# A two-branch gated-attention layer: phase 1 keeps the high and low parts of h in DRAM, and phases 2 and 3 load them

## The chip, the cores and the metric

The kernel runs on one core of one Trainium2 chip. The metric is the time of one launch on the device, in microseconds, as the median of several runs. The engines are named as in the profile: PE (matrix products) and PEld (loading its weights), DVE (VectorE), ACT (ScalarE), POOL (GpSimd), and SP (SyncE), whose queue issues nearly all transfers here. Each engine carries out its instructions in the order in which they stand in its queue, and waits where one of them needs something that another engine or a transfer has not delivered.

## The reference

One layer of a streaming encoder, for a prompt of 4096 tokens and 64 sample tokens, model width 1024, all in fp32. What is computed, cut to the core:

```python
mod = c @ w_ada + b_ada
shift, scale, gate = split(mod, 3)
h = rms_norm(x, g_pre) * (1 + scale) + shift
q_a, k_a, v_a, z_a, a_lr, q_h, f_h, i_h, z_h = split(h @ w_in)
o_a, s_a = chunked_gla(q_a, k_a, v_a, log_sigmoid(a_lr @ w_alpha + b_alpha) / 16, s_gla)
f = lb + (1 - lb) * sigmoid(f_h)
o_h, s_h = chunked_gla(silu(q_h), 1 - f, i_h, log(f), s_hgrn)
o_a = rms_norm(o_a, g_on_gla) * silu(z_a)
o_h = rms_norm(o_h, g_on_hgrn) * silu(z_h)
y = x + gate * rms_norm(concat(o_a, o_h) @ w_out, g_post)
```

So one input h feeds three groups of projections: those of the GLA branch, those of the HGRN2 branch, and the gate path z_h. The two recurrences carry a state from chunk to chunk.

## The kernel before, in words

A core does not hold all the split weights of `w_in` and `w_out` at once, so the work is done in three phases over the same tokens. The prompt is cut into 16 groups of 256 tokens, each of two tiles of 128; the 64 sample tokens ride with group 15 in phase 1 and with group 2 in phases 2 and 3, and that group has 320 columns.

An fp32 product is made of three matmuls on a high and a low part: hi·hi, hi·lo and lo·hi. `split` (L86) makes the two parts: ACT casts the source to the high part (L92), DVE subtracts it from the source to give the low part (L93). The same two lines split the weights, on DVE or on POOL. h of one group lies in SBUF as four tiles, each with two of the eight slices of the width: as fp32 in the tiles `hf` (pool of 4 buffers), and split in the tiles `hh` (pool of 5).

- **Setup** computes the modulation and makes h of group 0 directly as split tiles `h0` and as `hf`.
- **Phase 1** walks over the groups. For each it does the GLA projections (`proj_gla`, with L607 and L619 as the matmul lines). Woven between them, by generators with due times (`weave`), are the recurrence of the group before (`attend_group`) and the preparation of the next group: `x_load` brings x in 32 small loads (L486), `quad_norm` takes its norm (squares on ACT, L514; the sum over partitions as a small product on PE, L517; the scaling on DVE, L520), `x_turn` transposes it on DVE (L556) and applies scale and shift on ACT and DVE (L563, L565), which gives `hf`; then it stores `hf` to `h_d` in DRAM (L568). At the end of the group `split_h` (L579) makes the next group's `hh`.
- **Phase 2** walks over the groups again, with the HGRN2 projections and recurrence. `load_hf` (L572) brings `hf` back for the next group, and `split_h` splits it once more.
- **Phase 3** walks over the token tiles: the z projection (`z_tile`, L619), the turning of the gated outputs (L1300) and the out-projection (L1335). `load_hf` and `split_h` do the same a third time. Its weights `w_out` are loaded and split, on DVE, ACT and POOL, at the end of phase 2.

The order inside each engine's queue is set by a scheduler from the order of the code, the due times of the generators and its own estimate of lengths; the buffers of a pool decide when a tile may be written. Other lines that come up: L1156 scales a chunk's output on DVE and L1157 stores it to `oa_d` or `oh_d`; L850 updates the state S on DVE, which L823 on PE reads; L909 prepares K and staging tiles on DVE, which L766 and L956 read; L1263 loads `og`, the stored outputs, in phase 3, L1286 x, and L1351 stores y; L1253 loads w_out; L442 and L446 compute the gate rows in phase 2, from loads of L435.

Of the kernel before, what the change touches and what calls it, by code (L numbers as in the profile page):

```python
# [6 lines left out]
F32 = mybir.dt.float32  # L7
F32R = mybir.dt.float32r
# [20 lines left out]
class Kernel:  # L29
# [105 lines left out]
    def setup(self):  # L135
# [12 lines left out]
        for g, tl in enumerate(self.groups):  # L148
            self.h_d.append(dram.tile([P, KT, GROUP], F32, name=f"h_d{g}"))
            self.oa_d.append([dram.tile([r, 512], F32, name=f"oa_d{g}_{j}") for j, (_, _, r, _) in enumerate(tl)])  # L150
            self.oh_d.append([dram.tile([r, 512], F32, name=f"oh_d{g}_{j}") for j, (_, _, r, _) in enumerate(tl)])
        self.h_s = dram.tile([P, KT, self.dec], F32, name="h_s")
        self.gate_d = dram.tile([2, D], F32, name="gate_d")
# [62 lines left out]
    def first_group(self, ap, ada, w, rows):  # L216
# [110 lines left out]
        ada_sum(pa, parts.pop(0), [(1, 0), (1, 1)])  # L327
        self.hf = [self.hp.tile([P, 2, T], F32, name="hf", bufs=4) for _ in range(4)]
        nc.vector.tensor_copy(col[:, 16:], pr[:, 16:52])
# [6 lines left out]
        parts[1] = [ada_split(sts[1][0], nc.gpsimd)]  # L336
        self.h0 = [self.hp.tile([P, 2, 2, T], F32R, name="hh", bufs=5) for _ in range(4)]
        ada_turn(0, am)
# [149 lines left out]
    def x_norm(self, g, js):  # L488

        nc = self.nc  # L490
        ss = self.small.tile([P, 2], F32, name="x_ss")
        for i, j in enumerate(js):
            xt, r = self.xs[j], self.groups[g][j][2]
            junk = self.hp.tile([P, 2, GROUP], F32, name="hf", bufs=4).rearrange("p k c -> p (k c)")
# [27 lines left out]
    def x_turn(self, g):  # L522
# [3 lines left out]
        T = self.tokens(tl)  # L526
        self.hf = hf = [self.hp.tile([P, 2, T], F32, name="hf", bufs=4) for _ in range(4)]
        for tiles, cnd in (([0, 1], 0), ([2], 1)):
# [23 lines left out]
            for i in range(4):  # L552
# [13 lines left out]
                yield  # L566
        for i in range(4):
            nc.sync.dma_start(self.h_d[g][:, 2 * i : 2 * i + 2, :], hf[i][:, :, :GROUP])  # L568
            if len(tl) == 3:
                nc.sync.dma_start(self.h_s[:, 2 * i : 2 * i + 2, :], hf[i][:, :, GROUP:])  # L570

    def load_hf(self, g, tl):  # L572
        self.hf = [self.hp.tile([P, 2, self.tokens(tl)], F32, name="hf", bufs=4) for _ in range(4)]
        for i in range(4):
            self.nc.sync.dma_start(self.hf[i][:, :, :GROUP], self.h_d[g][:, 2 * i : 2 * i + 2, :])
            if len(tl) == 3:
                self.nc.sync.dma_start(self.hf[i][:, :, GROUP:], self.h_s[:, 2 * i : 2 * i + 2, :])

    def split_h(self):  # L579

        out = []
        T = self.hf[0].shape[2]
        for i in range(4):
            u = self.hp.tile([P, 2, 2, T], F32R, name="hh", bufs=5)
            self.split(u[:, 0], u[:, 1], self.hf[i])
            out.append(u)
        return lambda k: out[k // 2][:, :, k % 2]

# [791 lines left out]
    def run(self):  # L1380
# [11 lines left out]
        with ExitStack() as rec:  # L1392
            self.open_recurrence(rec)
            self.setup_late()
            for i in range(4):
                nc.sync.dma_start(self.h_d[0][:, 2 * i : 2 * i + 2, :], self.hf[i])
            h = lambda k: self.h0[k // 2][:, :, k % 2]
            S, Ss = [None], [t["state_gla"]]
# [10 lines left out]
            def prep_h(g, tl):  # L1409
                self.load_hf(g, tl)  # L1410
                yield

            for g in range(ng):
                prep = prep_x(g + 1) if g + 1 < ng else prep_h(0, self.groups2[0])
                sides = [(side, 12, 1, 18), (prep, 8, 0, 16) if g == 0 else (prep, 8, 7, 19)]
                if g == ng - 1:

                    sides.append((self.weights(W2["f"], C_FH, 512, "wu"), 10, 8, 18))
                    sides.append((self.weights(W2["q"], C_QH, 512, "wv"), 10, 20, 26))
                res = self.weave(self.proj_gla(g, h), sides)  # L1420
                h = self.split_h()
                side = self.attend_group(g, S, Ss, res, 2, 2, self.oa_d, t["new_gla_p"], t["new_gla_s"])
# [4 lines left out]
            for g in range(ng):  # L1427
# [113 lines left out]
```

## Time and profile before

| what | value |
|---|---|
| median of 3 runs | 2156.19 us (2154.54 to 2158.08) |
| the profiled execution | 2154.41 us, of which its span 2152.6 |
| granted PE clock, mean | 0.996 |
| bytes moved by DMA | 173.22 MB, mean 80 GB/s |
| phase 1, one group | 44.785 us |
| phase 3, one token tile | 17.3 us |

The profile is one execution, and all times in it are microseconds from its start, unless marked as nanoseconds. A row of a group names line, engine, operation and tiles, then the count, the busy time, the mean length of one in nanoseconds, and the idle time just ahead of these instructions with what ended most of it. A row of the list of waits names the waiting engine, its tile and line, what it waited for, and total, number and longest. In a timeline a bracket holds the idle time ahead of the row and what ended it.

### The profile page before, as it was taken

What the parts mean: (1) busy time and instruction counts of PE and PEld (TensorE: products, weight loads), DVE (VectorE), ACT (ScalarE), POOL (GpSimd) and SP (SyncE); (2) the same over time, 40 slices, a digit from 0 to 9 for tenths busy, and PEclk for the clock granted to TensorE, in tenths of its full rate; (3) what the DMA queues carried; (4) which work ended last, traced back from release to release, by engine and by line L of the source; (5) the groups of instructions that cost most, each with busy time, mean ns of one, the idle gap of its engine ahead of it and who ended that gap; (6) DMA issues with size and microseconds to landing.
All of it is one profiled execution on the core that took longest, in us unless ns stands there. A gap on an engine that the chain in (4) does not pass through costs nothing.

```text
span 2152.6 us, 44904 instructions
## 1 busy us (share of the span) xinstructions
PE 2108.6 (98%) x16574; PEld 1849.9 (86%) x16574; DVE 1492.5 (69%) x4851; ACT 996.1 (46%) x2960; POOL 239.8 (11%) x640
## 2 busy tenths in 40 slices
PE   8999999999999999999999999999989999999998
PEld 6888989889898888989999898999868888888887
DVE  6777767777677787677788777677995454545444
ACT  6666655665556664444444444444542222222212
POOL 3200010001100111110111111000330000000000
PEclk9999999999999999999999999999999999999999
DMA  9322222222222321112211111011343333333322
GB/s 274 102 63 71 61 56 50 72 66 58 55 50 64 118 87 39 38 33 71 66 50 50 31 31 50 31 31 48 98 150 132 118 123 108 127 117 131 108 100 88
DMA packets 218632, 173.22 MB, mean 80 GB/s; under 512 B 136236, under 2 KB 158224, under 8 KB 218412
## 3 DMA queue, kind: packets, MB, share of 16 engines
q1 hardware_dynamic: 218268, 170.08, 26.8%
q8 instruction: 131, 2.15, 0.4%
q14 instruction: 89, 0.73, 0.1%
q10 hardware_dynamic: 144, 0.26, 0.0%
HBM read 118.35 MB, written 51.93 MB: 79 GB/s over the span
## 4 chain that ended last, share of the span: by engine, by line
PE 85%; DVE 8%; ACT 4%; issue 1%; DMA 1%; POOL 0%; SPq 0%; DVEq 0%; ACTq 0%; POOLq 0%
PE ps_pj L619 23%; PE ps_pj L607 22%; PE ps_pj L1335 16%; PE ps_at L619 7%; PE ps_at L686 2%; PE ps_ms L839 2%; PE ps_o L823 2%; PE ps_o L818 2%; PE ps_at L956 2%; PE ps_at L766 1%; DVE wst L909 1%; PE ps_tp L793 1%; ACT A L776 1%; PE ps_tp L1300 1%; PE ps_ms L1300 1%
## 5 line engine op out<-in xcount | busy, mean ns | idle before, releaser
L619 PE MATMUL ps_pj<-wu,hh 128*128 128x512 f32 x1632 | 410.7, 398 | 4.3 <-DVE hh L93 3.4
L607 PE MATMUL ps_pj<-hh,wu 128*128 128x256 f32 (+1 forms) x2976 | 392.3, 287 | 0.0
L607 PEld LDWEIGHTS ps_pj<-hh,wu 128*128 128x128 f32 x2976 | 372.9, 191 | 4.9 <-issue 0.3
L619 PEld LDWEIGHTS ps_pj<-wu,hh 128*128 128x128 f32 x1632 | 296.4, 188 | 66.0 <-DVE hh L93 3.9
L607 PE MATMUL ps_pj<-hh,wv 128*128 128x256 f32 (+1 forms) x1536 | 214.1, 289 | 0.0
L607 PEld LDWEIGHTS ps_pj<-hh,wv 128*128 128x128 f32 x1536 | 192.5, 188 | 14.9 <-issue 12.9
L619 PE MATMUL ps_pj<-wv,hh 128*128 128x264 f32 x1464 | 199.3, 290 | 1.9 <-DVE wv L93 1.9
L619 PEld LDWEIGHTS ps_pj<-wv,hh 128*128 128x128 f32 x1464 | 184.2, 188 | 7.1 <-issue 2.3
L1340 ACT ACTIVATE sq<-ps_pj 128x512 bf16<-128x512 f32 (+1 forms) x66 | 39.4, 597 | 294.7 <-PE ps_pj L1335 293.2
L1335 PE MATMUL ps_pj<-wv,ogh 128*128 128x512 f32 x512 | 162.2, 397 | 0.0
L1335 PE MATMUL ps_pj<-wu,ogh 128*128 128x512 f32 x512 | 158.0, 390 | 0.0
L619 PE MATMUL ps_at<-wu,hh 128*128 128x512 f32 x672 | 157.4, 390 | 0.0
L92 ACT CAST hh<-hf 128x512 fp32r<-128x512 f32 (+1 forms) x188 | 117.3, 626 | 68.6 <-PE ps_pj L619 37.0
L619 PEld LDWEIGHTS ps_at<-wu,hh 128*128 128x128 f32 x672 | 126.0, 188 | 26.1
L1201 ACT ACTIVATE g<-ps_pj 128x256 f32<-128x256 f32 (+1 forms) x128 | 49.4, 386 | 200.2 <-PE ps_pj L607 199.8
L93 DVE TENSOR_TENSOR hh<-hf,hh 128x512 fp32r<-128x512 f32 (+1 forms) x188 | 132.5, 711 | 6.5 <-ACT hh L92 5.5
L909 DVE TENSOR_TENSOR wst<-wst,T 128x160 f32<-128x160 f32 (+4 forms) x480 | 118.4, 265 | 4.0
L1335 PEld LDWEIGHTS ps_pj<-wu,ogh 128*128 128x128 f32 x512 | 96.1, 188 | 20.8
L938 POOL COPY T<-T 128x16 f32<-128x16 f32 (+1 forms) x32 | 9.9, 309 | 931.4 <-DVE Qg L879 827.8
L1335 PEld LDWEIGHTS ps_pj<-wv,ogh 128*128 128x128 f32 x512 | 93.8, 188 | 19.1
L1335 PE MATMUL ps_pj<-wv,ogl 128*128 128x512 f32 x256 | 100.5, 393 | 0.0
L1335 PE MATMUL ps_pj<-wu,ogl 128*128 128x512 f32 x256 | 99.7, 390 | 0.0
(303 smaller groups left out, 3758.5 us busy)
## 6 DMA issues: line engine op xcount, KB each, us to landing
hf<-h_d SPq DMA_DIRECT2D x128, 256.0 KB
xt<-in_x_prompt_dram SPq DMA_DIRECT2D x36, 512.0 KB
h_d<-hf SPq DMA_DIRECT2D x64, 256.0 KB
out_y_prompt_dram<-y SPq DMA_DIRECT2D x31, 512.0 KB
xt<-in_x_prompt_dram SPq DMA_DIRECT2D x448, 32.0 KB
wst<-in_w_in_dram SPq DMA_DIRECT2D x36, 256.0 KB
ada_st<-in_w_ada_dram SPq DMA_DIRECT2D x32, 256.0 KB
oa_d<-e SPq DMA_DIRECT2D x32, 256.0 KB
```

What stands on the lines that cost most here:

```text
L92: self.nc.scalar.copy(hi, src)
L93: (eng or self.nc.vector).tensor_tensor(lo, src, hi.bitcast(F32), ALU.subtract)
L607: self.nc.tensor.matmul(ps[:, :T], a, b, start=i == 0, stop=i == n - 1)
L619: self.nc.tensor.matmul(ps[:r, : c1 - c0], a, b, start=kt == 0 and i == 0, stop=kt == KT - 1 and i == 2)
L686: nc.tensor.transpose(pt[:, i * P : (i + 1) * P], D[:, c + i, :], self.ident)
L818: nc.tensor.matmul(po[h], A[:, c * 4 + h, :], v, start=h < n, stop=St is None and h == 4 - n)
L823: nc.tensor.matmul(o, Q[rows[s], c * G + g, :], St[rows[s], g, :], start=NS == 2 and not apart and h == 1, stop=h == 4 - NS or h == 3 and ...
L839: nc.tensor.matmul(pd[s * w : (s + 1) * w, g, :], kc[:CL, g, s * w : (s + 1) * w], vs[c][:CL, h * P : (h + 1) * P], start=not apart, stop= ...
L909: nc.vector.tensor_tensor(parts(dst), parts(src), t.unsqueeze(3).to_broadcast(shape), ALU.mult)
L956: nc.tensor.matmul(pas[s][rows, g0 + g], K[rr, 2 * pr + g, rows], Yt[rr, o : o + P], start=True, stop=True)
L1201: nc.scalar.activation(sg, pf[:, :T], AF.Sigmoid)
L1335: nc.tensor.matmul(po[:r], a[:, kt, :r], b, start=m == 0, stop=m == 3 * KT - 1)
```

## The change

`h_d` and `h_s` now hold both parts of h, so they are twice as large. `x_turn` no longer stores `hf`. Instead `split_h(g)`, now called in phase 1 alone, stores the four split tiles right after it has made them (`keep_h`); those of group 0, which the setup has made, are stored by the same generator woven into the second half of group 0's projections. In phases 2 and 3 `load_h` loads split tiles: three of the next group's four ahead, and the fourth in `loaded`, when the projections that use the running group's tiles have been written down. `split_h` is not called there. The two pools `hf` and `hh` become one of seven buffers, in which one buffer holds either one split tile or two of the fp32 tiles; it takes the same room in SBUF.

```diff
-            self.h_d.append(dram.tile([P, KT, GROUP], F32, name=f"h_d{g}"))
+            self.h_d.append(dram.tile([P, 4, 2, 2, GROUP], F32, name=f"h_d{g}"))
...
-        for i in range(4):
-            nc.sync.dma_start(self.h_d[g][:, 2 * i : 2 * i + 2, :], hf[i][:, :, :GROUP])
-            if len(tl) == 3:
-                nc.sync.dma_start(self.h_s[:, 2 * i : 2 * i + 2, :], hf[i][:, :, GROUP:])
...
+    def hh_tile(self, T):
+        return self.hp.tile([P, 2, 2, T], F32R, name="hh", tag="hh", bufs=7)
+
+    def hf_pair(self, T):
+        return self.hp.tile([P, 4, T], F32, name="hf", tag="hh", bufs=7)
...
-    def split_h(self):
+    def split_h(self, g):
...
-            u = self.hp.tile([P, 2, 2, T], F32R, name="hh", bufs=5)
+            u = self.hh_tile(T)
             self.split(u[:, 0], u[:, 1], self.hf[i])
             out.append(u)
-        return lambda k: out[k // 2][:, :, k % 2]
+        for _ in self.keep_h(g, out):
+            pass
+        return self.by_kt(out)
+
+    def keep_h(self, g, tiles):
+
+        for i, u in enumerate(tiles):
+            u = u.bitcast(F32)
+            self.nc.sync.dma_start(self.h_d[g][:, i], u[..., :GROUP])
+            if u.shape[3] > GROUP:
+                self.nc.sync.dma_start(self.h_s[:, i], u[..., GROUP:])
+            yield
+
+    def load_h(self, g, tl, n):
+
+        T = self.tokens(tl)
+        for _ in range(n):
+            i = len(self.hnext)
+            u = self.hh_tile(T)
+            raw = u.bitcast(F32)
+            self.nc.sync.dma_start(raw[..., :GROUP], self.h_d[g][:, i])
+            if T > GROUP:
+                self.nc.sync.dma_start(raw[..., GROUP:], self.h_s[:, i])
+            self.hnext.append(u)
+
+    def loaded(self, g, tl):
+
+        self.load_h(g, tl, 4 - len(self.hnext))
+        tiles, self.hnext = self.hnext, []
+        return self.by_kt(tiles)
...
+                if g == 0:
+                    sides.append((self.keep_h(0, self.h0), 4, 10, 16))
...
-                h = self.split_h()
+                h = self.split_h(g + 1) if g + 1 < ng else self.loaded(0, self.groups2[0])
...
-                h = self.split_h()
+                g1 = (g + 1) % ng
+                h = self.loaded(g1, self.groups2[g1])
...
-                        hh = self.split_h()
+                        hh = self.loaded(g, self.groups2[g])
...
-                        self.load_hf(g + 1, self.groups2[g + 1])
+                        self.load_h(g + 1, self.groups2[g + 1], 3)
```

The change also moves instructions. Below the diff's first new function the line numbers of the changed kernel are 32 higher: L639 is L607 of before, L651 is L619, L988 is L956, L1189 is L1157, L882 is L850. Numbers on a row are the tile's shape and, after x, how many of the kind stand together.

PE, phase 1, a group in the steady part, before: the small product of the norm (L517) stands inside the first block of L956, ahead of the third of the projections that take the weights wv.

```order
L607 MATMUL ps_pj<-hh,wu 128x256 x24
L619 MATMUL ps_pj<-wv,hh 128x264 x24
L956 MATMUL ps_at<-wst,K_3841 32x128 x18
L517 MATMUL ps_tp<-q_ss,same 128x8
L956 MATMUL ps_at<-wst,K_3841 32x128 x14
L619 MATMUL ps_pj<-wv,hh 128x264 x48
L1070 MATMUL ps_ms<-ident,at_178 80x128
```

The changed kernel at the same product: it stands behind the whole first part of the recurrence, at the start of the projections that take wu.

```order
L855 MATMUL ps_o<-S,Qg 128x128
L855 MATMUL ps_ms<-S,Qg 128x128
L517 MATMUL ps_tp<-q_ss,same 128x8
L651 MATMUL ps_pj<-wu,hh 128x512 x3
L825 MATMUL ps_tp<-ident,K_3829 128x128 x2
L651 MATMUL ps_pj<-wu,hh 128x512 x3
L871 MATMUL ps_ms<-v,kT 64x128 x4
```

L517 has moved behind 72 products with wv, and 48 with wu are left behind it before the next group begins.

SP, phase 1, one group, before: stores of h (L568), of the recurrence's outputs (L1157), and the loads of x (L486) of the group after the next.

```order
L568 DMA h_d_131<-hf 128x512 x2
L486 DMA xt<-in_x_prompt_dram 32x8x32
L568 DMA h_d_131<-hf 128x512
L486 DMA xt<-in_x_prompt_dram 32x8x32
L568 DMA h_d_131<-hf 128x512
L486 DMA xt<-in_x_prompt_dram 32x8x32 x4
L1157 DMA oa_d_0_122<-e 128x512
L486 DMA xt<-in_x_prompt_dram 32x8x32 x6
L1157 DMA oa_d_1_123<-e 128x512
L486 DMA xt<-in_x_prompt_dram 32x8x32 x20
```

The same stretch of the changed kernel, where L598 stores a split tile:

```order
L598 DMA h_d_141<-hh 128x1024
L486 DMA xt<-in_x_prompt_dram 32x8x32 x2
L1189 DMA oa_d_0_132<-e 128x512
L598 DMA h_d_141<-hh 128x1024 x3
L1189 DMA oa_d_1_133<-e 128x512
L486 DMA xt<-in_x_prompt_dram 32x8x32 x30
```

Thirty of the 32 loads of x now stand behind the last three stores of h and behind both stores of the outputs.

DVE, the end of group 15's recurrence at the start of phase 3, before: the last updates of the state (L850), with the splits of later groups' h (L93) and the gated outputs (L1242, L1292) ahead of them.

```order
L93 TENSOR_TENSOR hh<-hf,hh 128x640
L878 TENSOR_TENSOR K_21138<-K_21138,T_22115 128x4x64
L879 TENSOR_TENSOR Qg<-Qg,T_22115 128x4x64
L878 TENSOR_TENSOR K_21138<-K_21138,T_22115 128x4x64
L879 TENSOR_TENSOR Qg<-Qg,T_22115 128x4x64
L881 TENSOR_TENSOR T_22158<-T_22115 128x8
L1242 TENSOR_TENSOR e<-ps_pj,e 128x512
L93 TENSOR_TENSOR hh<-hf,hh 128x640 x2
L1292 TENSOR_TENSOR xt<-xt,e 128x512
L93 TENSOR_TENSOR hh<-hf,hh 128x640
L850 SCALAR_TENSOR_TENSOR S<-S,T_22158,ps_ms 128x128 x4
```

The changed kernel at the same update (L882):

```order
L913 TENSOR_TENSOR T_21864<-T_21675 128x16
L1274 TENSOR_TENSOR e<-ps_pj,e 128x512
L910 TENSOR_TENSOR K_20914<-K_20914,T_21864 128x4x64
L911 TENSOR_TENSOR Qg<-Qg,T_21864 128x4x64
L910 TENSOR_TENSOR K_20914<-K_20914,T_21864 128x4x64
L911 TENSOR_TENSOR Qg<-Qg,T_21864 128x4x64
L913 TENSOR_TENSOR T_21907<-T_21864 128x8
L882 SCALAR_TENSOR_TENSOR S<-S,T_21907,ps_ms 128x128 x4
```

The splits of h have left the queue, and L1292's product (L1324 there) stands some forty rows earlier.

More of the change, by code (lines that the diff above doesn't have):

```diff
@@ L148, in setup @@
         for g, tl in enumerate(self.groups):
-            self.h_d.append(dram.tile([P, KT, GROUP], F32, name=f"h_d{g}"))
+            self.h_d.append(dram.tile([P, 4, 2, 2, GROUP], F32, name=f"h_d{g}"))
             self.oa_d.append([dram.tile([r, 512], F32, name=f"oa_d{g}_{j}") for j, (_, _, r, _) in enumerate(tl)])
             self.oh_d.append([dram.tile([r, 512], F32, name=f"oh_d{g}_{j}") for j, (_, _, r, _) in enumerate(tl)])
-        self.h_s = dram.tile([P, KT, self.dec], F32, name="h_s")
+        self.h_s = dram.tile([P, 4, 2, 2, self.dec], F32, name="h_s")
         self.gate_d = dram.tile([2, D], F32, name="gate_d")
@@ L327, in first_group @@
         ada_sum(pa, parts.pop(0), [(1, 0), (1, 1)])
-        self.hf = [self.hp.tile([P, 2, T], F32, name="hf", bufs=4) for _ in range(4)]
+        self.hf = self.hf_tiles(T)
         nc.vector.tensor_copy(col[:, 16:], pr[:, 16:52])
@@ L336, in first_group @@
         parts[1] = [ada_split(sts[1][0], nc.gpsimd)]
-        self.h0 = [self.hp.tile([P, 2, 2, T], F32R, name="hh", bufs=5) for _ in range(4)]
+        self.h0 = [self.hh_tile(T) for _ in range(4)]
         ada_turn(0, am)
@@ L493, in x_norm @@
             xt, r = self.xs[j], self.groups[g][j][2]
-            junk = self.hp.tile([P, 2, GROUP], F32, name="hf", bufs=4).rearrange("p k c -> p (k c)")
+            junk = self.hf_pair(GROUP)[:, :2].rearrange("p k c -> p (k c)")
             nc.scalar.activation(
@@ L526, in x_turn @@
         T = self.tokens(tl)
-        self.hf = hf = [self.hp.tile([P, 2, T], F32, name="hf", bufs=4) for _ in range(4)]
+        self.hf = hf = self.hf_tiles(T)
         for tiles, cnd in (([0, 1], 0), ([2], 1)):
@@ L566, in x_turn, with hf_tiles, by_kt @@
                 yield
-        for i in range(4):
-            nc.sync.dma_start(self.h_d[g][:, 2 * i : 2 * i + 2, :], hf[i][:, :, :GROUP])
-            if len(tl) == 3:
-                nc.sync.dma_start(self.h_s[:, 2 * i : 2 * i + 2, :], hf[i][:, :, GROUP:])
[L572 to L577, printed above, removed]
-    def split_h(self):
+    def hh_tile(self, T):
+        return self.hp.tile([P, 2, 2, T], F32R, name="hh", tag="hh", bufs=7)
+    def hf_pair(self, T):
+        return self.hp.tile([P, 4, T], F32, name="hf", tag="hh", bufs=7)
+    def hf_tiles(self, T):
+        return [t[:, 2 * i : 2 * i + 2] for t in [self.hf_pair(T) for _ in range(2)] for i in range(2)]
+    @staticmethod
+    def by_kt(tiles):
+        return lambda k: tiles[k // 2][:, :, k % 2]
+    def split_h(self, g):
         out = []
@@ L1394, in run @@
             self.setup_late()
-            for i in range(4):
-                nc.sync.dma_start(self.h_d[0][:, 2 * i : 2 * i + 2, :], self.hf[i])
-            h = lambda k: self.h0[k // 2][:, :, k % 2]
+            h = self.by_kt(self.h0)
+            self.hnext = []
             S, Ss = [None], [t["state_gla"]]
@@ L1409, in prep_h @@
             def prep_h(g, tl):
-                self.load_hf(g, tl)
+                self.load_h(g, tl, 3)
                 yield
```

## The prediction

> **What bounds the kernel now.** I read the page first: its head, the busy times and the chain that ended last.
>
> ```profile
> span 2152.6 us, 44904 instructions
> PE 2108.6 (98%) x16574; PEld 1849.9 (86%) x16574; DVE 1492.5 (69%) x4851; ACT 996.1 (46%) x2960; POOL 239.8 (11%) x640
> PE 85%; DVE 8%; ACT 4%; issue 1%; DMA 1%; POOL 0%; SPq 0%; DVEq 0%; ACTq 0%; POOLq 0%
> ```
>
> TensorE (PE) is busy for 2108.6 of 2152.6 us, and 85% of the last chain is its own work. The change takes no matmul away, so at most the 44 us in which PE stands can be won, and a good part of those lies in the setup. Then I asked for the busy time by stretches, to see in which stage PE stands: a phase-2 stretch, the two stretches round the start of phase 3, and one inside phase 3.
>
> ```profile
> 1080.00:1134.00 54.00, 53.81 (x479) 48.79 (x478) 43.69 (x148) 24.78 (x69) 9.46 (x26) 1.00 0.14 46
> 1512.00:1566.00 54.00, 50.38 (x409) 44.02 (x409) 49.96 (x136) 28.34 (x74) 16.26 (x26) 0.97 0.33 100
> 1566.00:1620.00 54.00, 46.88 (x327) 37.41 (x326) 47.42 (x126) 27.24 (x68) 20.41 (x33) 0.97 0.52 169
> 1900.00:1954.00 54.00, 54.00 (x252) 44.71 (x251) 28.05 (x77) 12.92 (x28) 0.00 (x0) 1.00 0.39 127
> ```
>
> The columns are the length, then the busy time of PE, PEld, DVE, ACT and POOL, the granted clock, the DMA share and GB/s. In phase 2 PE stands 0.2 of 54 us, in phase 3 not at all; only the stretch between them is loose (3.6 and 7.1 us), and there VectorE (DVE) is as busy as PE. The list of PE's waits says for whom:
>
> ```profile
> PE ps_tp L517 <- ACT sqx L514: 6.6, 11, 0.8
> PE ps_o L823 <- DVE S L850: 3.7, 1, 3.7
> PE ps_pj L619 <- DVE hh L93: 3.4, 1, 3.4
> PE ps_tp L1300 <- DMA og<-oa_d: 3.1, 1, 3.1
> PE ps_at L766 <- ACT A L776: 2.7, 4, 1.2
> PE ps_at L766 <- DVE K L909: 2.2, 11, 0.3
> PE ps_pj L619 <- ACT K L1036: 0.9, 1, 0.9
> ```
>
> Columns: total, times, longest. Two of them recur in nearly every phase-1 group (6.6 + 2.2 us over 11 groups, 0.8 us each); the next three single ones lie at the start of phase 3 (3.7 + 3.4 + 3.1 = 10.2 us).
>
> **The change part by part.** *What it removes.*
>
> ```profile
> L92 ACT CAST hh<-hf 128x512 fp32r<-128x512 f32 (+1 forms) x188 | 117.3, 626 | 68.6 <-PE ps_pj L619 37.0
> L93 DVE TENSOR_TENSOR hh<-hf,hh 128x512 fp32r<-128x512 f32 (+1 forms) x188 | 132.5, 711 | 6.5 <-ACT hh L92 5.5
> hf<-h_d SPq DMA_DIRECT2D x128, 256.0 KB
> h_d<-hf SPq DMA_DIRECT2D x64, 256.0 KB
> ```
>
> Splits fall from 188 to 60, all left in phase 1. That is 128 casts of 0.626 us, 80 us of ScalarE (ACT), and 128 subtractions of 0.711 us, 91 us of DVE, out of phases 2 and 3. *What it adds:* the 128 loads become 512 KB and the 64 stores too, 33.6 + 16.8 MB more. Two queues of work get lighter that PE hardly waits for; so the question is stage by stage.
>
> *Phase 3, at 0.* Two consecutive steps of a token tile:
>
> ```profile
> 1640.70 5.44 PE ps_at L619 x24
> ...
> 1647.02 10.98 PE ps_pj L1335 x48
> ```
>
> One tile takes 5.44 + 0.44 + 0.44 + 10.98 = 17.3 us, all PE; the order inside phase 3 keeps PE's rows. The removed work hid behind PE (DVE busy 28 of 54 us). The DMA share of 0.39 grows by 256 KB for each of four loads in 34.6 us, 30 GB/s on 127, which still leaves half of the queues' time. If that cover failed, each tile would wait on its load; I see no row for it.
>
> *Phase 2, −1.* PE's rows are identical, and 0.2 us per 54 us over 760 us, 3 us, is all that can be won; I take a third. What is late next is the fourth h tile. Three are loaded a group ahead, the fourth only when the slot of the running group's first tile is free, which is when the last projection has passed it, 18 matmuls before the group's end. The rates:
>
> ```profile
> 211.09 5.47 PE ps_pj L619 x24
> 216.55 4.31 PE ps_pj L607 x36
> ...
> 664.40 4.31 PE ps_pj L607 x36
> ```
>
> 18 x 5.47/24 = 4.1 us, and the next group reads that tile after 18 narrow matmuls, 18 x 4.31/36 = 2.2 us: 6.3 us from issue to need. The trace of before has no such load. Bounds: 512 KB at the 169 GB/s of the row 1566:1620 take 3.1 us, at 274 GB/s (the first stretch on the page, the highest) 1.9; the landing of small x loads (below) lies within 4.9 us. So 1.9 to 8.0 us; I take 4 to 5, nearer to the bare transfer, since phase 2 has a DMA share of only 0.14. That is inside the 6.3, with little to spare.
>
> *Phase 1, −5.* The last fence also gives the period: (664.40 − 216.55)/10 = 44.785 us a group. What sets L517's wait is the x loads on SP:
>
> ```profile
> 209.25 3.19 SPq L486 DMA_DIRECT2D xt<-in_x_prompt_dram  x5
> 214.00 0.33 SPq L1157 DMA_DIRECT2D oa_d<-e  x1
> 214.36 15.84 SPq L486 DMA_DIRECT2D xt<-in_x_prompt_dram  x23
> ```
>
> ```profile
> 235.13 0.39 PE L517 MATMUL ps_tp<-q_ss,same 128*128 128x8 f32 x2 [0.33 <-ACT sqx L514]
> ```
>
> ```profile
> 257.67 0.33 SPq L1157 DMA_DIRECT2D oa_d<-e  x1
> ```
>
> SP issues them at 0.64 to 0.69 us each, the last ends at 230.20, and L517 comes 4.9 us later. By the order L517 moves behind 72 matmuls with wv and the first part of the recurrence, and DVE no longer scales x (L520) between L927 and K of L909, so both recurring waits go: −0.8 us. Against that, the transposes, the casts and three of the four L93 now come in the last 14 us before the next group. The new group reads the second split tile after 6 narrow matmuls (0.7 us), the third and fourth 0.7 us and 1.4 us on, while three L93 last 2.1 us from whenever the last L565 allows them. No row shows this; it can be 0 (all early) or the whole 2.1 us. I take 0.4, because PE's 14.4 us (48 wide matmuls, 10.9, plus 3.5 of attention) are about what that chain takes now. So −0.4 over 13 groups, −5; ends 13 x −0.8 = −10 and 13 x (2.1 − 0.8) = +17.
>
> *The queues that steps are moved past.* h stores now wait for L93 instead of L565, and 30 of 32 x loads stand behind them and behind both oa_d stores. So a loop closes: L517, the second oa_d store, 30 loads, landing, L514, L517. Before, L517 to that store was 257.67 − 235.13 = 22.5 us; behind a chain that starts late and has less queued in front I take 20. 30 loads are 19.1 to 20.7 us. Landing and squares are 4.9 us before, though part of that is a queue on ACT; the floor I put at 2, an estimate of mine from the difference of these rows. Ends: 41.1 and 48.1 us; PE's need is 44.785 − 0.8 + 0.4 = 44.4. I take 20 + 20.7 + 2.5 = 43.2, just inside. This is the weakest number here.
>
> *The start of phase 3, −7.* PE's waits there, what DVE did ahead of the second, and POOL beside it:
>
> ```profile
> 1556.53 1.47 PE L619 MATMUL ps_pj<-wu,hh 128*128 128x512 f32 x4 [3.44 <-DVE hh L93]
> 1595.38 2.08 PE L823 MATMUL ps_o<-S,Qg 128*128 128x128 f32 x8 [3.75 <-DVE S L850]
> 1613.68 0.63 PE L1300 MATMUL ps_tp<-ident,og 128*128 128x128 f32 x4 [3.06 <-DMA og<-oa_d]
> ```
>
> ```profile
> 1583.21 0.82 DVE L93 TENSOR_TENSOR hh<-hf,hh 128x640 fp32r<-128x640 f32 x1
> ...
> 1588.16 3.42 DVE L93 TENSOR_TENSOR hh<-hf,hh 128x640 fp32r<-128x640 f32 x2
> 1591.51 1.75 DVE L1292 TENSOR_TENSOR xt<-xt,e 128x512 f32<-128x512 f32 x1
> 1593.18 1.88 DVE L93 TENSOR_TENSOR hh<-hf,hh 128x640 fp32r<-128x640 f32 x1
> 1594.99 1.11 DVE L850 SCALAR_TENSOR_TENSOR S<-S,T,ps_ms 128x128 f32<-128x128 f32 x4
> ```
>
> ```profile
> 1587.81 3.09 POOL L93 TENSOR_TENSOR wu<-wst,wu 128x512 fp32r<-128x512 f32 x2 [0.19 <-ACT wu L92]
> 1591.24 3.15 POOL L93 TENSOR_TENSOR wu<-wst,wu 128x512 fp32r<-128x512 f32 x2 [0.34 <-DMA wst<-in_w_out_dram]
> ```
>
> The first wait is for a split that no longer exists: −3.4. In the second, 3.42 + 1.88 = 5.3 us of splits stood in DVE's queue ahead of L850, more than the 3.75 us waited: −3.7. The third is a load behind a chain of stores; I leave it at 3.1. Sum −7. On the other side, the fourth load of group 0 now stands on SP behind w_out's loads, whose buffers free as POOL and DVE split; that can hand back up to 4 us. Ends −3 and −10.
> The rows show one 128x640 subtraction at 0.82 us alone and 1.71 us (3.42/2) while POOL splits. The Trainium skill, "SBUF — State Buffer", section "SBUF: two separate sides", says that a DVE operation with two SBUF inputs and a GpSimd operation that reads SBUF exclude each other for a whole instruction; by that the operations that move up take over the blocking, some 0.9 us each, and this part would be about −5 rather than −7. The trace's 1.75 us of L1292 agrees with it.
>
> *Edges, −2.* The wait on K of L1036 (0.9, group 1) and the one of 1.2 us on A of L776 at the end of phase 1 stand where splits and stores are moved; I take both, ends 0 and −2.1.
>
> Sum: 0 − 1 − 5 − 7 − 2 = −15. The profiled execution took 2154.41 us (1.8 around its span) and becomes 2139.4; its median of three is 2156.19, so 2141.
>
> **The rivals.** (B) Phase 1 gives nothing: the 0.8 us come back as a wait on hh of L93. For it speaks that split and need lie within a microsecond. −10: 2146. (C, slower) The x loop becomes the bound of phase 1: stores of h, of oa_d and 30 x loads are one queue, each waiting for the one ahead. It decides from 44.4 us on. At 46.5 us a group costs 1.7 more than now, 13 x 1.7 = +22, −10 elsewhere: +12, 2168. For it: the upper end of 48.1. Against: both long rows contain waits that the order takes out. (D) The fourth load lands late in phase 2, at 7.4 us against 6.3: 15 x 1.1 = +17, −14: 2159. Against it: the DMA share of 0.14. The Trainium skill, "DMA: Bandwidth & Descriptors", section "Anatomy of one DMA", gives 2.0 us and the bytes at 436 GB/s, so an estimated 3.2 us for 512 KB; no run here shows one. (E) The change does not reach the end: the start of phase 3 stays bound by POOL's weight splits and the loads, and phase 1 gives nothing: −1, 2155.
>
> **How the numbers follow.** Forecast (A) 0.50, B 0.17, C 0.13, D 0.06, E 0.14. A measurement here can tell about 0.2%, 4.3 us: faster is under 2151.9, slower over 2160.5. A and B are faster: 0.67. E and half of D are the same: 0.17. C and the other half of D are slower: 0.16. The range: low, phase 1 at −10, phase 2 at −3, the start of phase 3 at −10, edges −2, and a few microseconds for the 44 us that PE stands now: 2128. High: E, D and the milder third of C (+7): 2163. About 1 in 10 is left out at each end.
>
> **What would show it.** Right: in the list of PE's waits L517 <- L514 and L766 <- K of L909 are gone or small, L619 <- hh L93 and L823 <- S of L850 are gone at the start of phase 3, phase 1's period is 44.3 to 44.5 us, phase 2 and phase 3 keep their PE rows and their pitch, and DVE's busy time falls by about 91 us. Wrong: a period over 44.785 us with L517 waiting longer on the x loads (C), a wait of L607 on hh from L93 of 0.8 us or more in every group (B), a wait on hh from h_d at each phase-2 group's start (D), or the three waits at the start of phase 3 under other names (E).

## The result, and the profile after

The changed kernel takes 2174.12 us (median of 6, 2172.18 to 2176.62), the kernel before 2156.41 (6 runs, 2154.46 to 2158.34): a ratio of 1.0083, 95% interval 1.0073 to 1.0093. So it is slower by 0.8%, where the forecast was 0.7% faster. The profiled execution took 2176.62 us, 2174.8 of it the span. The head of its page:

```profile
span 2174.8 us, 44468 instructions
...
PE 2121.8 (98%) x16574; PEld 1855.7 (85%) x16574; DVE 1410.7 (65%) x4723; ACT 915.6 (42%) x2832; POOL 239.6 (11%) x640
...
PE 83%; DVE 9%; ACT 5%; issue 1%; DMA 1%; POOL 1%; SPq 0%; DVEq 0%; POOLq 0%; ACTq 0%
```

The busy time of DVE fell by 82 us and that of ACT by 80 (forecast 91 and 80); the row of L93 itself went from 132.5 to 39.6 us, 93 less. (Rows overlap a little in the trace, so they do not add up to the busy time.) PE, with the same 16574 matmuls, is busy 13 us longer; the stretches at half the clock and the order of its own products, both below, are part of that. The removed work itself, and the transfers that took its place:

```profile
L93 DVE TENSOR_TENSOR hh<-hf,hh 128x512 fp32r<-128x512 f32 (+1 forms) x60 | 39.6, 693 | 0.6 <-ACT hh L92 0.6
```

```profile
hh<-h_d SPq DMA_DIRECT2D x128, 512.0 KB
h_d<-hh SPq DMA_DIRECT2D x64, 512.0 KB
```

So the change does what it says. Where the time went is seen by following one landmark through both traces, the first narrow projection of a group (L607 before, L639 now). The steps between them:

| stretch | before, us | after, us | difference | in the prediction |
|---|---|---|---|---|
| to group 1 | 81.54 | 89.22 | +7.7 | part of edges, 0 to −2 |
| groups 1 to 13 | 582.70 | 589.18 | +6.5 | −5 |
| groups 14 and 15, to phase 2 | 103.09 | 112.19 | +9.1 | the rest of edges |
| first group of phase 2 | 48.47 | 51.43 | +3.0 | 0 |
| rest of phase 2 | 687.87 | 688.14 | +0.3 | −1 |
| start of phase 3, to its third tile | 143.11 | 138.70 | −4.4 | −7 |
| from there to the end | 505.86 | 505.89 | 0.0 | 0 |

The differences sum to 22.2, while the medians differ by 17.7: the profiled execution of after is 2.5 above its median, that of before 2.0 under its own. The steady groups, on the chain that ended last:

```profile
225.99 4.31 PE ps_pj L639 x36
...
678.56 4.31 PE ps_pj L639 x36
```

(678.56 − 225.99)/10 = 45.257 us a group, against 44.785. PE's waits over the whole span (total, times, longest):

```profile
PE ps_at L798 <- ACT A L808: 9.2, 16, 1.3
PE ps_pj L358 <- ACT hh L269: 4.5, 7, 0.7
PE ps_ms L1102 <- DVE at L1097: 3.0, 1, 3.0
PE ps_at L718 <- DVE dd L724: 3.0, 3, 1.6
PE ps_o L235 <- DVE c L93: 2.9, 1, 2.9
PE ps_pj L639 <- ACT hh L92: 2.8, 1, 2.8
PE ps_at L798 <- DVE K L941: 2.2, 11, 0.3
PE ps_tp L1332 <- DMA og<-oa_d: 2.0, 1, 2.0
PE ps_at L718 <- DVE nwt_u L81: 2.0, 1, 2.0
...
PE ps_tp L517 <- ACT sqx L514: 0.3, 1, 0.3
```

The wait of L517 on the squares, 6.6 us in 11 waits before, is gone. In its place stands L798 (L766 before) on A, 2.7 in 4 before and 9.2 in 16 now. The other new rows are mostly single waits of 2 to 3 us: in the setup (L235 on c), in group 0 (L1102) and in group 15 (L718 on nwt_u, L639 on hh); of the three waits of L718 on dd one, of 1.6 us, lies in the first group of phase 2 and one at the start of phase 3. The row of L358, in the setup, stood at 3.5 us in 6 waits before. No row of this list waits for h_d.

Stretches inside phase 2 and phase 3 (length; busy time of PE, PEld, DVE, ACT, POOL; granted clock; DMA share; GB/s):

```profile
1100.00:1154.00 54.00, 53.80 (x480) 49.02 (x480) 41.27 (x134) 22.56 (x65) 6.28 (x18) 1.00 0.27 88
...
1920.00:1974.00 54.00, 54.00 (x251) 44.78 (x250) 23.91 (x74) 9.39 (x21) 0.00 (x0) 1.00 0.48 166
```

PE is as full there as before (53.81 and 54.00 of 54 us then), and DVE has less to do: work was taken away that hid behind PE.

### The profile page after: what moved, and what is told of

The parts are those of the page before. It is cut to its first block, busy times and chain, and to the rows that moved or that the text cites. A ratio compares the mean times of both kernels' runs of the same rounds, so it can differ in the third digit from the quotient of the medians.

```text
span 2174.8 us, 44468 instructions
## 1 busy us (share of the span) xinstructions
PE 2121.8 (98%) x16574; PEld 1855.7 (85%) x16574; DVE 1410.7 (65%) x4723; ACT 915.6 (42%) x2832; POOL 239.6 (11%) x640
## 4 chain that ended last, share of the span: by engine, by line
PE 83%; DVE 9%; ACT 5%; issue 1%; DMA 1%; POOL 1%; SPq 0%; DVEq 0%; POOLq 0%; ACTq 0%
PE ps_pj L639 22%; PE ps_pj L651 20%; PE ps_pj L1367 16%; PE ps_at L651 7%; PE ps_at L718 2%; PE ps_ms L871 2%; PE ps_o L850 2%; PE ps_o L855 2%; PE ps_at L988 2%; ACT A L965 2%; PE ps_at L798 1%; DVE wst L941 1%; PE ps_tp L825 1%; ACT A L808 1%; DVE Ac L959 1%
## 5 line engine op out<-in xcount | busy, mean ns | idle before, releaser
L651 PE MATMUL ps_pj<-wu,hh 128*128 128x512 f32 x1632 | 415.6, 401 | 0.0
L639 PE MATMUL ps_pj<-hh,wu 128*128 128x256 f32 (+1 forms) x2976 | 393.6, 288 | 2.8 <-ACT hh L92 2.8
L639 PEld LDWEIGHTS ps_pj<-hh,wu 128*128 128x128 f32 x2976 | 374.8, 192 | 7.7 <-ACT hh L92 3.0
L651 PEld LDWEIGHTS ps_pj<-wu,hh 128*128 128x128 f32 x1632 | 296.5, 189 | 60.9 <-issue 3.5
L639 PE MATMUL ps_pj<-hh,wv 128*128 128x256 f32 (+1 forms) x1536 | 214.1, 289 | 0.0
L639 PEld LDWEIGHTS ps_pj<-hh,wv 128*128 128x128 f32 x1536 | 192.5, 188 | 14.9 <-issue 12.9
L651 PE MATMUL ps_pj<-wv,hh 128*128 128x264 f32 x1464 | 197.5, 289 | 1.6 <-DVE wv L93 1.6
L651 PEld LDWEIGHTS ps_pj<-wv,hh 128*128 128x128 f32 x1464 | 183.3, 188 | 6.8 <-ACT e L1086 2.2
L651 PE MATMUL ps_at<-wu,hh 128*128 128x512 f32 x672 | 157.1, 389 | 0.0
L651 PEld LDWEIGHTS ps_at<-wu,hh 128*128 128x128 f32 x672 | 126.1, 188 | 26.1
L941 DVE TENSOR_TENSOR wst<-wst,T 128x160 f32<-128x160 f32 (+4 forms) x480 | 119.1, 264 | 4.2
L965 ACT ACTIVATE A<-Ac,member 128x128 f32<-128x128 f32 x256 | 80.2, 390 | 40.2 <-DVE Ac L959 40.1
L882 DVE SCALAR_TENSOR_TENSOR S<-S,T,ps_ms 128x128 f32<-128x128 f32 x186 | 58.4, 340 | 51.1 <-PE ps_ms L871 50.9
```

Of the source, the lines that this page charges most:

```text
L639: self.nc.tensor.matmul(ps[:, :T], a, b, start=i == 0, stop=i == n - 1)
L651: self.nc.tensor.matmul(ps[:r, : c1 - c0], a, b, start=kt == 0 and i == 0, stop=kt == KT - 1 and i == 2)
L882: nc.vector.scalar_tensor_tensor(Sn[:, g, :], St[:, g, :], T[:, c * G + g, 0:1], pd[:, g, :], ALU.mult, ALU.add)
L941: nc.vector.tensor_tensor(parts(dst), parts(src), t.unsqueeze(3).to_broadcast(shape), ALU.mult)
L965: nc.scalar.activation(Ah[:, :, 32 * b : 32 * b + 32], Ach, AF.Copy, scale=self.member[:CL, 8 + b : 9 + b])
```

## The experiments

The theory after the result: on SP's queue most of a group's 32 loads of x stand behind the stores of split h, which wait for the splits; so everything that follows from x comes late, and the losses are what this lateness and the new order cost. Three rivals: the shared pool does it; the doubled bytes do it; the x loop sets the period (the slower rival of the prediction, C). Medians are of 4 to 12 runs each; those of the kernel before beside them are 2157.0 to 2157.6 us. Ratios are to the kernel before.

### The shared pool alone

e1 is the kernel before with only the pool of seven buffers.

```diff
-        self.hf = [self.hp.tile([P, 2, T], F32, name="hf", bufs=4) for _ in range(4)]
+        self.hf = self.hf_tiles(T)
...
-            u = self.hp.tile([P, 2, 2, T], F32R, name="hh", bufs=5)
+            u = self.hh_tile(T)
...
```

> The kernel before with only the shared pool of seven buffers: h is still stored as fp32 by x_turn, loaded and split again in phases 2 and 3, so bytes and splits are those of before. Theory P (places): the pool alone lets the norm of group 1's x run early in group 0, where its two scalings stand on DVE ahead of weight splits; that part, about 4 us with the half clock behind PE's wait, comes, and nothing else: 2160 us (2158 to 2164), phase 1's period as before, 44.8. Rival G (the coarser pool holds the tiles longer and so costs all of phase 1): 2170 or more, with the period at 45.2. Rival B (the 50 MB more of traffic slow the engines or the loads everywhere): nothing is added here, 2156.

Measured: 2158.19 us, ratio 1.0003 (0.9994 to 1.0012). The pool as such costs nothing that can be told. Its profile does have the 3.0 us wait of group 0 (there L1079 on `at` of L1074).

### The norm of group 1 later

In all kernels with the shared pool group 1's norm gets its buffer early, and its two scalings (L500) stand on DVE ahead of splits of weights that PE waits for. e2 ties that norm to a buffer that comes free later.

```diff
-            junk = self.hf_pair(GROUP)[:, :2].rearrange("p k c -> p (k c)")
+            junk = (self.hf[3] if g == 1 else self.hf_pair(GROUP)[:, :2]).rearrange("p k c -> p (k c)")
```

> The changed kernel, with one edit: the scratch tile for the squares of group 1's x is the last fp32 tile of group 0, so that this norm can't start before that tile has been read. Theory P: PE's wait of 3.1 us in group 0 falls to about 1 us, and the half clock behind it goes: 4 us less than the changed kernel, 2170 (2168 to 2172). Rivals G and B: 2174, no change.

Measured: 2175.89 us, ratio 1.0094 (1.0080 to 1.0107), so no better than after. The wait on L1097 went, and another of 4.2 us (L651 on ACT's Xg of L1058) came at the same place. The early norm sets which wait stands there, not that one does; the loss of group 0 was not removed by it.

### The sample tokens first

Group 15 also prepares the sample tokens, whose x is loaded into one of the two buffers of the prompt's x. e3 gives the sample its own buffer and puts its loads and its norm ahead.

```diff
...
+                    if len(self.groups[g]) == 3:
+                        self.x_load(g, [2])
                     self.x_load(g, [0, 1])
+                    if len(self.groups[g]) == 3:
+                        self.quad_norm(g, [2])
```

> The changed kernel, with one edit: the sample tokens' x goes into a free buffer of the h pool and is loaded and normed with group 15's x, ahead of its two prompt tiles, in place of waiting for one of the two x buffers. Theory P: the waits of 2.1 and 2.9 us and the half clock at the start of group 15 go, 7 to 10 us less than the changed kernel: 2165 (2162 to 2168); the period of the other groups stays 45.25. Rival G: the pool is even fuller here, so 2174 or more. Rival B: 2174.

Measured: 2172.62 us, ratio 1.0072 (1.0059 to 1.0085). The stretch of group 14 fell from 52.87 to 42.97 us, and that of group 15 rose from 59.32 to 66.78. Eight more loads stood ahead of the prompt's, whose product of the norm came at 714.34; what follows from it then held ACT and PE in group 15 (PE's timeline of e3):

```profile
723.84 0.71 PE L850 MATMUL ps_o<-v,A 128*128 128x128 f32 x4 [2.04 <-ACT sq L890]
```

A miss against the expected 2165: the loss moved from one group to the next. What is put first on this queue makes the rest late.

### The same stores, a group later

e4 leaves pool, bytes and splits as in after, and moves only the place of the stores on SP: h of each group is stored in the second half of that group's own projections, as the change did for group 0 alone.

```diff
-        for _ in self.keep_h(g, out):
-            pass
+        self.kept = out
...
-                if g == 0:
-                    sides.append((self.keep_h(0, self.h0), 4, 10, 16))
+                sides.append((self.keep_h(g, self.h0 if g == 0 else self.kept), 4, 10, 16))
```

> The changed kernel, with the stores of the split h woven into the second half of the next group's projections for every group, as the changed kernel does for group 0 alone. Bytes, pool and splits are those of the changed kernel; only the place of the stores on SP differs, and with it the loads of x start earlier and L517 stands ahead of the projections with wv again. Theory P: the period returns to 44.8 or somewhat below (5 us), and the sample tile's loads come 15 us earlier (8 us): 2160 (2154 to 2165). Rivals G and B: 2174 (2172 to 2177).

Measured: 2152.18 us, ratio 0.9981 (0.9972 to 0.9990): 22 us under after, and the first version under the kernel before. SP's queue in a steady group, after:

```profile
406.66 1.64 SPq L598 DMA_DIRECT2D h_d<-hh  x3
411.04 0.32 SPq L1189 DMA_DIRECT2D oa_d<-e  x1
411.41 35.62 SPq L486 DMA_DIRECT2D xt<-in_x_prompt_dram  x30
```

And e4:

```profile
388.43 4.49 SPq L486 DMA_DIRECT2D xt<-in_x_prompt_dram  x7
394.33 0.33 SPq L1188 DMA_DIRECT2D oa_d<-e  x1
394.70 7.33 SPq L486 DMA_DIRECT2D xt<-in_x_prompt_dram  x10
402.44 2.86 SPq L597 DMA_DIRECT2D h_d<-hh  x4
420.44 10.23 SPq L486 DMA_DIRECT2D xt<-in_x_prompt_dram  x15
```

The 32 loads of one group begin where SP has waited some 15 us for DVE's transposes (L556) to free the buffers of xt. In after this wait lies inside the row of 30 loads, which lasts 35.62 us: 27 of them belong to the group whose first five stand ahead of the three stores, and three to the next group. So 27 of 32 loads stand behind these stores, not the thirty that the order seemed to show. The stores of h alone hold them little; the longest wait there is the one ahead of the second store to oa_d (408.30 to 411.04), behind which 27 loads of a group now stand in place of 20. In e4 the wait ends at 420.44, and all 32 loads of a group (15, 7 and 10) stand ahead of the stores of h, whose data has been ready for long. Its chain gives the period:

```profile
219.66 4.31 PE ps_pj L638 x36
...
664.73 4.31 PE ps_pj L638 x36
```

(664.73 − 219.66)/10 = 44.507 us, 0.75 under after and 0.28 under before. Bytes, pool and the work of each engine are after's, so neither bytes nor pool explain the loss; the place of the stores on SP's queue does.

### The stores on ACT's queue

```diff
-            self.nc.sync.dma_start(self.h_d[g][:, i], u[..., :GROUP])
+            self.nc.scalar.dma_start(self.h_d[g][:, i], u[..., :GROUP])
```

> The changed kernel with its stores of the split h issued from ACT's queue in place of SP's; bytes, pool, splits and the place of the stores in the program are those of the changed kernel. Theory Q (on SP's queue the loads of x stand behind stores that wait for the last split, so the norm comes late and group 15's sample tokens later still): SP is free for x, L517 stands ahead of the projections with wv as in the kernel that stores a group later, phase 1's period is 44.5 and group 15 begins without a wait: 2154 (2150 to 2159). Rival W (it is the place in time of the 512 KB writes, right at a group's end, whatever the queue): 2172 to 2176.

Measured: 2163.80 us, ratio 1.0035 (1.0023 to 1.0047), slower than the expected 2150 to 2159, with a period of 45.01 us. Nine of the ten groups in it take 44.80 us and one 46.93, part of it at half the clock (see the end). SP is free of these stores, and the sample's loss is nearly gone (45.73 us for group 14's stretch). But PE's wait on ACT's A (L798 on L808) grows to 13.4 us in 14. A store that waits for DVE's L93 now stands in ACT's queue and can hold its copies; that this makes the wait longer is not shown.

### A group later, but at the group's start

e6 is e4 with the stores in the first steps of the group. The edit is shown against e4.

```diff
-                sides.append((self.keep_h(g, self.h0 if g == 0 else self.kept), 4, 10, 16))
+                sides.append((self.keep_h(g, self.h0 if g == 0 else self.kept), 4, *((10, 16) if g == 0 else (1, 5))))
```

> The kernel that stores a group later, with the stores woven into steps 1 to 5 of the next group's projections in place of 10 to 16, so that they stand ahead of the loads of x again: on SP the order is three stores, the second output store, then 30 loads of x, as in the changed kernel. Theory Q: the time of the changed kernel, 2174 (2171 to 2177), with a period of 45.25. Rival S (what helped was that the split tiles and their stores are no longer tied to the group's end in the program, not the order on SP): 2152 to 2158.

Measured: 2171.36 us, ratio 1.0072 (1.0057 to 1.0086), period 45.26 us: after's time, from e4's code with two numbers changed. The cost is the place.

### The kernel before with late stores

e7 has before's pools, bytes and later splits, but its stores stand where the change puts them and wait for L93. They keep only the low part of h and leave out the rest, so phases 2 and 3 compute from that part alone, with the same instructions.

```diff
-        for i in range(4):
-            nc.sync.dma_start(self.h_d[g][:, 2 * i : 2 * i + 2, :], hf[i][:, :, :GROUP])
...
+        for i in range(4 if g is not None else 0):
+            self.nc.sync.dma_start(self.h_d[g][:, 2 * i : 2 * i + 2, :], out[i].bitcast(F32)[:, 1, :, :GROUP])
...
```

> The kernel before, with its fp32 stores of 256 KB taken from the low parts, after the split, in place of from hf ahead of it (phases 2 and 3 then compute from the low part of h alone): bytes, pools and splits are those of before, only the stores now wait for L93, so that 25 of 32 loads of x stand behind them and L517 moves 5 us later. Theory Q: part of the loss comes back in the kernel before: a period of 44.9 to 45.3 and a wait at group 15's start, 2165 (2160 to 2172). Rival P (pool) and rival B (bytes): 2157, no change.

Measured: 2162.93 us, ratio 1.0025 (1.0014 to 1.0035). The sample's loss is there without the change's pool and loads: 50.67 us for group 14's stretch (45.11 before), with PE waiting ahead of group 15:

```profile
713.17 1.09 PE L686 MATMUL ps_at<-ident,A 128*128 128x128 f32 x4 [3.03 <-DVE A L724]
```

But its ten steady groups take 444.66 us, 3.2 less than before. So late loads of x by themselves do not make the steady groups slow: that part of the theory fell.

### Two halves

e8 stores h of groups 12 to 15 a group later and the others as after does; e9 is its counterpart.

```diff
-        for _ in self.keep_h(g, out):
-            pass
+        self.kept = out
+        if not (g >= 12):
+            for _ in self.keep_h(g, out):
+                pass
...
```

> The changed kernel; only the h of groups 12 to 15 is stored a group later (steps 10 to 16), the h of groups 1 to 11 at the group's end as in the changed kernel. By the order the norm's L517 stands late up to group 11 and comes forward then, and the small L517 of the sample tokens stands ahead of the last 24 products with wu again. Theory Q, two separate terms: the groups up to 11 keep the period of 45.25 (about 5 us lost against before), group 15 begins without a wait (9 us won back): 2164 (2161 to 2167). Rival R (one cause, the late norm of every group, adds up and is paid out at the end): both terms come back only together, 2172 to 2176.

> The counterpart: the h of groups 1 to 11 is stored a group later, that of groups 12 to 15 at the group's end. L517 stands early up to group 11 and falls back to the end of the wv products by group 15; the sample tokens' L517 stands 5 products ahead of group 15. Theory Q: the period of 44.5 up to group 11, and most of group 15's loss, 5 to 9 us: 2159 (2156 to 2162). Rival R: 2152 to 2155, since nothing has added up by then.

Measured: e8 2161.42 us, ratio 1.0022 (1.0012 to 1.0031); e9 2156.74 us, ratio 0.9992 (0.9983 to 1.0001). e8 keeps after's 45.3 us a group up to group 10 and has 44.65 us in group 14's stretch; e9 has 44.5 us a group, and in groups 14 and 15 about half of the sample's loss (47.98 and 59.65 us, 4.5 over before). So the steady groups and the sample are two separate losses with one cause, the place of the stores.

### Where the norm stands, with the stores of e4

In e4 the preparation of the next group begins at step 7 of its weaving. e10, e11 and e12 begin it at steps 9, 11 and 8, for all but the last groups. The edit of e10 against e4:

```diff
-                sides = [(side, 12, 1, 18), (prep, 8, 0, 16) if g == 0 else (prep, 8, 7, 19)]
+                sides = [(side, 12, 1, 18), (prep, 8, 0, 16) if g == 0 else (prep, 8, 9 if g < 11 else 7, 19)]
```

> The kernel that stores a group later; the next group's x is brought and normed from step 9 of the projections on in place of step 7, for the groups up to 10, so that L517 stands a little inside the last 36 products with wv, behind the block of L956. Theory D (the wait of 0.9 us on A of L808 in every group of the kernel that stores a group later comes because the norm's scaling, two times 1.2 us on DVE, stands just ahead of the chain that makes A): the wait goes and the period is 44.0, 2147 (2144 to 2150). Rival N (the chain to A takes that long whatever stands ahead of it): the period stays 44.5, 2152.

> The same with step 11 for the groups up to 11; L517 stands 24 products with wv later still. Theory D: 44.0 again, 2147 (2144 to 2151). Rival N: 2152. If lateness itself cost time, this would be slower than the kernel with step 9, toward the 45.25 of the changed kernel.

> The same with step 8 for the groups up to 11; L517 stands in the middle of the first 24 products with wv, ahead of the block of L956. Theory D: the scaling then falls together with the chain's start, so this lies between step 7 and step 9: 44.2 to 44.5, 2150 (2147 to 2153). Rival N: 2152.

Measured: e10 2151.62 us, ratio 0.9974 (0.9964 to 0.9983); e11 2154.17, 0.9983 (0.9975 to 0.9992); e12 2152.31, 0.9980 (0.9971 to 0.9988). All periods lie between 44.4 and 44.5 us, where theory D expected 44.0 for e10 and e11, and the intervals overlap with e4's. A later norm does not lengthen the period; this too speaks against lateness as the cost in the steady groups. Nor do PE's waits alone decide it: between 200 and 600 us PE waits 5.5 us in e4, nearly all on ACT's A; in e11 that wait is gone and 0.7 us of waits are left, at the same period.

## Why the prediction was wrong

**The failed step: the sum has no term for group 15.** The forecast priced the recurring waits and left "edges" for waits that it could see. The largest single loss, +9.1 us in groups 14 and 15, had no row before, since the chain of the sample tokens fitted. The sample's loads in before:

```profile
694.33 5.14 SPq L486 DMA_DIRECT2D xt<-in_x_sample_dram  x8
```

After:

```profile
716.55 3.82 SPq L486 DMA_DIRECT2D xt<-in_x_sample_dram  x6
```

They need the buffers that the prompt's x leaves, so the late prompt is followed by a sample later still: 22 us after their old place, though group 14 itself began only 14 us later than before (678.40 against 664.24). PE before, where the sample's L517 comes ahead of 23 wide matmuls of the group:

```profile
703.51 0.28 PE L517 MATMUL ps_tp<-q_ss,same 128*128 128x2 f32 x2
703.65 5.51 PE L619 MATMUL ps_pj<-wu,hh 128*128 128x512 f32 x23
```

And after, with nothing left to put between:

```profile
725.52 0.38 PE L517 MATMUL ps_tp<-q_ss,same 128*128 128x2 f32 x2 [0.32 <-ACT sqx L514]
...
727.87 0.63 PE L718 MATMUL ps_at<-ident,A 128*128 128x128 f32 x4 [1.97 <-DVE nwt_u L81]
...
731.27 2.06 PE L639 MATMUL ps_pj<-hh,wu 128*128 128x320 f32 x6 [2.77 <-ACT hh L92]
```

The chain L517, L520, L556, L563, L92 stands open: waits of 2.0 and 2.8 us, two smaller ones of 0.5 and 0.3 ahead of them, and after them a stretch at half the clock. The waits are 5.6 of the 9.1 us; most of the rest fits the half clock (see the end). e7 shows it in before's code, e4 and e8 take it away by the place of the stores alone (44.91 and 44.65 us).

**Phase 1, −5: the sign of the steady groups was wrong, +0.47 us a group.** That L517's wait goes was right. The 0.4 us priced for hh of L93 never came: no such row stands in the list. What came instead, in the steady groups of before (200 to 660 us):

```profile
PE ps_tp L517 <- ACT sqx L514: 6.1, 10, 0.8
```

and of after:

```profile
PE ps_at L798 <- ACT A L808: 5.7, 11, 0.6
```

One wait took the place of the other, for about the same sum. The second wait that the forecast counted as recurring in phase 1 (L766 on K of L909, 2.2 us in 11) was misread: the list is over the whole span, the stretch of phase 1 has no such row, and after still has it, 2.2 in 11, as L798 on K of L941. Removing it could give nothing. And the forecast priced waits alone: what a new order costs inside PE's own work had no term. The time from one PE instruction's start to the next, summed by tile over ten steady groups, shows it (us a group; a wait counts with the products ahead of it; lines of before):

| PE's products | before | after | e4 | e7 |
|---|---|---|---|---|
| L956, in before with L517's wait inside | 1.97 | 1.09 | 1.09 | 1.10 |
| with wv, and in after and e4 the wait on A | 12.50 | 12.96 | 13.23 | 12.54 |
| Qg with K (L766) and L1070 | 0.74 | 1.20 | 1.18 | 0.84 |
| S with Qg (L823) | 1.29 | 1.71 | 1.29 | 1.92 |
| wide ones with wu | 11.49 | 11.54 | 11.16 | 11.27 |
| all others | 16.78 | 16.75 | 16.55 | 16.80 |
| one group | 44.79 | 45.26 | 44.51 | 44.47 |

So the gain at L517 came, 0.88 us, and three rows of 0.42 to 0.46 us each took it back. One of them is the products of S with Qg. In before, those for `ps_o` and `ps_ms` alternate, and each pair begins within 0.01 us; eight take 0.64 us (431.13 to 431.77):

```profile
431.13 0.37 PE L823 MATMUL ps_o<-S,Qg 64*128 64x128 f32 x1
431.13 0.37 PE L823 MATMUL ps_ms<-S,Qg 64*128 64x128 f32 x1
...
431.77 0.66 PE L839 MATMUL ps_ms<-v,kT 128*64 128x128 f32 x8
```

A group has two such sets of eight. In after the second is parted by other products, and its first two, both for `ps_o`, take 0.42 us by themselves (446.63 to 447.05):

```profile
446.63 0.49 PE L855 MATMUL ps_o<-S,Qg 64*128 64x128 f32 x2
447.05 0.71 PE L850 MATMUL ps_ms<-v,A 128*128 128x128 f32 x4
```

e4 has all of them in pairs again, and e7 parts one set wholly. The runs show that the place of the stores on SP decides, through the order that follows from it on the other engines; no run changed one of these orders alone, and e7 pays most for S with Qg and is yet no slower than e4. Of the +6.5 us in groups 1 to 13, these ten groups are 4.7; the rest lies in groups 1 to 3.

**Rival C had the sign and the place, not the mechanism.** It said the loop of stores and 30 loads (27, as the queue shows) would become the bound. After's SP waits up to 15.5 us, 202.2 in all, for DVE's L556 to free a buffer of xt, so the queue has time to spare. A loop that set the period would have PE's L517 wait on the loads, and L517 waits 0.3 us in all. The range's upper end took C in by a third, and its chance was 0.13. Rival B's wait on hh of L93 is in no row of the steady groups, so B fell too.

**Edges, −2, became +7.7 up to group 1.** Three parts: PE's 3.0 us wait on L1097 (0.7 in before), a setup wait of 2.9 us on c that before's execution does not have, and a slower clock, on which see below; 2.3 + 2.9 leaves 2.5 us for the clock, for four transposes of x (L541) that moved here from group 1, and the rest. The second need not come from the change: e7, with before's pools and lines, has 2.4 us of it (e1 1.6, e4 2.1, e2 4.4). The first comes with the shared pool (e1), not with the stores (e7 has 0.7). Of the two waits that the term counted, that on K of L1036 went, and that on A at the end of phase 1 stayed, at 1.3 us.

**Phase 2's first group, priced at 0, costs 3.0.** All profiles of kernels that load split h have it (50.5 to 51.4 us, in e4 too, against 48.5 in before, e1 and e7). PE and DVE there, in e4:

```profile
775.84 0.30 PE L717 MATMUL ps_at<-ident,xt 128*64 128x128 f32 x1 [1.77 <-DVE dd L723]
```

```profile
775.29 0.16 DVE L912 TENSOR_TENSOR xt<-xt 128x2 f32<-128x2 f32 x1 [2.83 <-POOL xt L971]
775.37 0.41 DVE L723 TENSOR_REDUCE dd<-ps_at 64x4 f32<-64x256 f32 x1
```

In before dd (L692, at 772.25) stands ahead of that small product in DVE's queue. In e4 the small product stands ahead of dd, which PE needs, and waits 2.83 us for POOL. So DVE's order is another once the splits of h are out of its queue; that their absence alone brings this order about, no run shows.

**What was right.** The rest of phase 2 (+0.3; −1 forecast) and phase 3 (0.0). The fourth load, the 4-to-5-us guess against 6.3, was not waited for in after, so rival D fell. (The section of the Trainium skill's "DMA: Bandwidth & Descriptors" that the prediction names there gives its figure for transfers issued from GpSimd; these are issued from SP, and the profiles give no landing time for them, so that estimate stays untested.) The same step of two consecutive tiles in phase 3, on the chain:

```profile
1662.80 5.44 PE ps_at L651 x24
...
1680.13 5.44 PE ps_at L651 x24
```

1680.13 − 1662.80 = 17.3 us a tile, as before. The start of phase 3 gave −4.4 in these two profiles, inside the ends of −3 and −10; over all eleven profiles with split loads it takes 136.9 to 139.8 us, against 140.2 to 147.0 in the three without. Both waits that were to go went; in their place, after:

```profile
1585.46 0.63 PE L718 MATMUL ps_at<-ident,A 128*128 128x128 f32 x4 [1.21 <-DVE dd L724]
...
1610.53 1.12 PE L825 MATMUL ps_tp<-ident,K 128*128 128x128 f32 x4 [1.12 <-DVE K L910]
1633.40 0.63 PE L1332 MATMUL ps_tp<-ident,og 128*128 128x128 f32 x4 [2.03 <-DMA og<-oa_d]
```

Part of the 7.2 us comes back as waits of about 1 us on DVE, which is why −7 was too much, and the −5 of the sentence on the Trainium skill was nearer; whether for the reason given there, these runs do not say.

## What to carry to other kernels

A store that waits for late data holds everything behind it on its issuing queue; put it where its data has long been ready, and look first at what stands behind it. Then compare the order of the busiest engine's own work before and after: it was full here, and yet the same products took 0.47 us a group longer or 0.28 less by their order and waits. Before pricing a later start, follow the longest chain that must still fit before the next group, in the odd group too (here the one with the sample tokens), not only the waits that a steady group shows; and place each row of a whole-span list in its stage before counting it. e10 and e4, with the stores a group later, beat both kernels by little: 0.26% and 0.19% under the kernel before, 1.0% under the change.

## What the runs showed of the hardware

**The clock after a short wait.** At PE's waits of about 3 us in group 0 and ahead of group 15 the granted clock fell to half (the column behind POOL's busy time), in stretches of after:

```profile
78.00:84.00 6.00, 5.50 (x17) 4.39 (x18) 2.79 (x12) 1.95 (x5) 0.00 (x0) 0.50 0.24 95
...
730.00:736.00 6.00, 4.73 (x17) 4.61 (x18) 6.00 (x18) 4.32 (x10) 3.83 (x5) 0.50 0.52 153
```

and after the same 3.0 us wait in e1:

```profile
76.00:82.00 6.00, 5.44 (x31) 4.29 (x32) 3.39 (x13) 2.65 (x8) 0.00 (x0) 1.00 0.12 44
```

In e4 that stretch has 0.72. In after the stretches of 6 us on both sides of 78:84 have 0.97 and 0.96, so the clock was half for about 6.8 us; that is 3.4 us of lost work, an estimate from these figures. So a wait of 3 us can cost about twice itself, and it does not each time. A shorter wait can be enough: in e5 PE's only idle time from 648 to 651 us is one wait of 1.27 us on A, and the clock is 0.50 from 651.5 to 654.5. The Trainium skill, "TensorE: Matmul & The Clock Gate", section "What's actually happening", puts the change to half the clock at an idle window of about 3.4 us; here it came with waits of 1.3 to 3.0 us, in some profiles and not in others.

**A small subtraction held by POOL.** The split of c, 128x16, took 2.32 us in after on DVE:

```profile
10.76 2.32 DVE L93 TENSOR_TENSOR c<-col,c 128x16 fp32r<-128x16 f32 x1
```

beside this one on POOL:

```profile
10.71 2.34 POOL L93 TENSOR_TENSOR ada_l<-ada_st,ada_h 128x1024 fp32r<-128x1024 f32 x1 [3.98 <-ACT ada_h L92]
```

In before DVE's began at 9.95, 0.03 us ahead of POOL's 2.39 us at 9.98, and took 0.17. Here POOL began 0.05 us earlier than DVE, and DVE's small operation lasted as long as POOL's whole one: this is the setup wait on c. In e1, e2 and e7, which have the wait too, it lasted 2.32 to 2.34 us. The section "SBUF: two separate sides" of the Trainium skill's "SBUF — State Buffer", which lets two such operations exclude each other, agrees with these rows.
